# First pool group's gates as plain products in place of a seven-product scheme, in a two-layer trunk kernel

## Chip, cores and metric

The kernel runs on one core of a Trainium2 chip. The metric is the device time of one execution in microseconds (us). The kernel before took 920.03 us, the median of three runs (919.65 to 921.34).

## The reference, cut to what matters

The input is 512 tokens of width 1024, in float32. An even layer (matrix memory and stick-breaking attention) is followed by an odd layer, a pooling mixer. The change lies in the odd layer alone:

```python
def odd_layer(x, pre_g, post_g, w_in, pool_w, pool_scale, w_out):
    h = rmsnorm(x, pre_g)
    u = h @ w_in                                  # (512, 1024) @ (1024, 4096)
    p, z = u[..., :2048], u[..., 2048:]
    pooled = multiscale_pool(p in 4 groups of 512 channels)   # windows 2, 4, 8, 16: mean less the token
    mixed = einsum('bsgc,gce->bsge', pooled, pool_w)          # 512 x 512 per group
    y = (mixed * pool_scale * silu(z)) @ w_out
    return x + rmsnorm(y, post_g)
```

Here z holds the gates: 512 columns for each of the four groups.

## The kernel before, in words

Activations are kept transposed, 128 channels by 512 tokens, so that a product takes 128 weight columns as the stationary operand of TensorE and streams the tokens. Every float32 operand is split in two: a rounded half made by ScalarE (ACT, line 71) and the rest made by VectorE (DVE, line 72). `mm3` (lines 93 to 97) then issues three matmuls for each 128 by 128 block of weights. The normalised activations of the odd layer are `hTh` and `hTl`; the unsplit ones are kept in `y32`.

The odd layer goes through the four pool groups one after the other (loop at line 734). For a group it does five things:

- the projections p: two loads of 256 weight columns, four tiles of 128 columns, each tile eight blocks times three matmuls (`project2`, `col_proj`). In group 0 each tile is done in two token halves, since the second half of the tokens is normalised late (line 745). The results go to tiles `win` through line 748;
- the pooling: shifted sums on DVE (line 763), a small repair of the first tokens on GpSimd (POOL, lines 768 and 769), the rest on DVE (line 770), and the split in `pph` and `ppl`;
- the gates z: for each pair of column tiles `strassen2` (lines 688 to 732) forms the 256 by 512 result from seven products of half size (128 columns, half the channels, 256 tokens) in place of eight. It needs sums of the weights (lines 696 to 700, on DVE, then split) and sums of the activations;
- the load and split of the mixing weights `pw` (lines 783 and 784);
- the mixing itself, four tiles `mx` (lines 785 to 791), and line 792, which scales and gates.

The activation sums d3, d1, n2 and t4 are made once by `hidden_sums` (lines 672 to 686), four 128 by 1024 operations on DVE and four splits, and serve all eight gate pairs. Group 0 calls it behind its projections (line 749).

The program is written in this order, but a scheduler sets the order on each engine: it moves instructions by what they depend on and by its own cost estimates. Each engine then works strictly in its order. Loads are issued by SyncE's queue (SP) in order too; a load waits until its buffer is free. There are two load buffers (`w32`), four pairs of split weights (`wh`, `wl`), two banks `pj` for projections, and two banks `ac` for the mixing. Plain projections use the `pj` banks; `strassen2` uses one `pj` bank and two others (line 712).

Of the kernel before, what the change touches and what calls it, by code (L numbers as in the profile page):

```python
# [7 lines left out]
AF = mybir.ActivationFunctionType  # L8
# [28 lines left out]
def body(nc, tc, x, pre_g, post_g, w_in, conv, b_i, b_f, hn_g, w_out, w_in_c, pool_w,  # L37
# [6 lines left out]
    with base as base, psum as psum, dram as dram:  # L44
# [157 lines left out]
        with tc.tile_pool(name="att", bufs=1) as at:  # L202
# [374 lines left out]
            for u in range(HB // 2):  # L577
                pair = heads_b(u)
                stick_pair(pair, ((sc, sc), (xa, xb)))
                z = raw2(ZB + 256 * u, f"zb{u}")  # L580
# [46 lines left out]
        with tc.tile_pool(name="odd", bufs=1) as od:  # L627
# [44 lines left out]
            def hidden_sums():  # L672
                raw = {}
                b11, b21, b12, b22 = quarter(0, 0), quarter(1, 0), quarter(0, 1), quarter(1, 1)
                for n in ("d3", "d1", "n2", "t4"):
                    raw[n] = ws(f"raw_{n}").rearrange("p a n -> p (a n)").rearrange("p (a n) -> p a n", a=4)
                    hs[n] = [big(f"{n}{e}", F32R).rearrange("p (a n) -> p a n", a=4) for e in "hl"]
                    if n == "d3":
                        V.tensor_tensor(raw[n], b22, b12, op=ALU.subtract)
                    elif n == "d1":  # L680
                        V.tensor_tensor(raw[n], b11, b12, op=ALU.subtract)
                    elif n == "n2":
                        V.scalar_tensor_tensor(raw[n], raw["d3"], -1.0, b11, op0=ALU.mult, op1=ALU.subtract)
                    else:
                        V.scalar_tensor_tensor(raw[n], raw["n2"], -1.0, b21, op0=ALU.mult, op1=ALU.subtract)
                    split(raw[n], *hs[n])

            def strassen2(src, name, dsts, silu=False):

                w = load(lambda t: [(nc.sync, t, src)], 8, 256, name)  # L690
                a11, a12, a21, a22 = (w[:, 4 * k:4 * k + 4, m * P:m * P + P]
                                      for m in range(2) for k in range(2))
                sums = [ws(f"ws{i}_{name}") for i in range(2)]
                s1, s2, s3, s4 = sums[0][:, 4:], sums[0][:, :4], sums[1][:, :4], sums[1][:, 4:]
                first = halves(w[:, :, :P], f"{name}_a")
                V.tensor_tensor(s1, a21, a22, op=ALU.add)
                V.tensor_tensor(s2, s1, a11, op=ALU.add)
                second = halves(sums[0], f"{name}_b")
                V.tensor_tensor(s3, a11, a21, op=ALU.add)
                V.tensor_tensor(s4, a12, s2, op=ALU.add)  # L700
                third = halves(sums[1], f"{name}_c")
                fourth = halves(a22, f"{name}_d")

                def product(ps, wt, k0, b, start, stop):
                    (wh, wl), (bh, bl) = wt, hs[b]
                    for k in range(4):
                        mm3(ps, (wh[:, k0 + k], wl[:, k0 + k]), (bh[:, k], bl[:, k]),
                            start and k == 0, stop and k == 3, skip_group_check=True)

                def part(i): return od.tile([P, 256], F32, tag="part", bufs=4, name=f"pt{i}_{name}")  # L710

                pa, pb, pe = (f(f"ps{n}_{name}")[:, :256] for f, n in ((pj, "a"), (xa, "b"), (xb, "e")))
                t1, t2, t5 = part(1), part(2), part(5)
                product(pa, first, 0, "11", True, True)
                A.activation(t1, pa, AF.Copy)
                product(pb, first, 4, "21", True, True)
                V.tensor_tensor(dsts[0][:, :256], pb, t1, op=ALU.add)
                product(pa, second, 0, "n2", False, True)
                A.activation(t2, pa, AF.Copy)
                product(pe, second, 4, "d1", True, True)  # L720
                A.activation(t5, pe, AF.Copy)
                product(pa, third, 0, "d3", False, True)
                V.scalar_tensor_tensor(dsts[1][:, 256:], pa, -1.0, t5, op0=ALU.mult, op1=ALU.subtract)
                product(pe, third, 4, "22", False, True)
                V.tensor_tensor(dsts[0][:, 256:], pe, t2, op=ALU.add)
                product(pa, fourth, 0, "t4", False, True)
                if silu:
                    act(dsts[0], dsts[0], AF.Silu)
                    act(dsts[1][:, 256:], dsts[1][:, 256:], AF.Silu)
                    act(dsts[1][:, :256], pa, AF.Silu, scale=-1.0)  # L730
                else:
                    A.activation(dsts[1][:, :256], pa, AF.Copy, scale=-1.0)

            for g, w in enumerate(WINDOWS):
                pooled = []
                cur4 = []
                for j in range(4):
                    c = 4 * g + j
                    cur = od.tile([P, 16 + S], F32, tag="win", bufs=6, name=f"p_{c}")
                    G.memset(cur[:, :16], 0.0)  # L740
                    cur4.append(cur)
                wsrc = [w_in_c[0, :, 512 * g + 256 * i:512 * g + 256 * i + 256] for i in range(2)]
                if g == 0:
                    wj = [t() for i in range(2) for t in col_load(wsrc[i], f"p{g}{i}")]
                    for j, n0 in ((j, n0) for n0 in (0, 256) for j in range(4)):
                        ps = pj(f"ps_p{4 * g + j}_{n0}")
                        col_proj(wj[j], ps, n0, n0 + 256)
                        A.activation(cur4[j][:, 16 + n0:16 + n0 + 256], ps[:, n0:n0 + 256], AF.Copy)
                    hidden_sums()
                else:  # L750
                    for i in range(2):
                        for j, ps in enumerate(project2(wsrc[i], f"p{g}{i}")):
                            A.activation(cur4[2 * i + j][:, 16:], ps, AF.Copy)
                for j in range(4):
                    c = 4 * g + j
                    cur = cur4[j]
                    p32 = cur[:, 16:]
                    sh = 1
                    while sh < w:
                        nx = od.tile([P, 16 + S], F32, tag="win", bufs=6, name=f"p_{c}_{sh}")  # L760
                        if 2 * sh < w:
                            G.memset(nx[:, :16], 0.0)
                        V.tensor_tensor(nx[:, 16:], cur[:, 16:], cur[:, 16 - sh:16 + S - sh],  # L763
                                        op=ALU.add)
                        cur, sh = nx, 2 * sh
                    sm = cur[:, 16:]
                    e = w - 1
                    G.tensor_tensor(sm[:, :e], sm[:, :e], invc[:, :e], op=ALU.mult)  # L768
                    G.tensor_tensor(sm[:, :e], sm[:, :e], p32[:, :e], op=ALU.subtract)
                    V.scalar_tensor_tensor(sm[:, e:], sm[:, e:], 1.0 / w, p32[:, e:], op0=ALU.mult,  # L770
                                           op1=ALU.subtract)
                    ph = od.tile([P, S], F32R, tag="phi", bufs=5, name=f"pph{c}")
                    pl = od.tile([P, S], F32R, tag="plo", bufs=5, name=f"ppl{c}")
                    split(sm, ph, pl)
                    pooled.append((ph, pl))
                sz = []
                for i in range(2):
                    pair = [od.tile([P, S], F32, tag="sz", bufs=4, name=f"sz{4 * g + 2 * i + j}")
                            for j in range(2)]
                    strassen2(w_in_c[0, :, 2048 + 512 * g + 256 * i:2304 + 512 * g + 256 * i],  # L780
                              f"z{g}{i}", pair, True)
                    sz.extend(pair)
                w4 = load(lambda t: [(nc.sync, t, pool_w[0, g])], 4, 512, f"pw{g}")
                pw = [halves(w4[:, 2 * i:2 * i + 2], f"pw{g}{i}") for i in range(2)]
                for e in range(4):
                    c = 4 * g + e
                    ps = ac(f"mx{c}")
                    for k in range(4):
                        wh, wl = pw[k // 2]
                        mm3(ps, (wh[:, k % 2, e * P:e * P + P], wl[:, k % 2, e * P:e * P + P]),  # L790
                            pooled[k], k == 0, k == 3)
                    V.scalar_tensor_tensor(y32[:, c], ps, psc(c), sz[e], op0=ALU.mult, op1=ALU.mult)
# [44 lines left out]
```

## Time and profile before

| what | value |
|---|---|
| runs, median (lowest to highest) | 920.03 us (919.65 to 921.34) |
| the profiled execution's own time | 920.03 us |
| its span, first to last instruction | 918.0 us |
| TensorE matmul busy (share of the span) | 900.2 us (98%) |
| VectorE busy | 581.1 us (63%) |
| ScalarE busy | 491.2 us (54%) |
| GpSimd busy | 76.1 us (8%) |
| mean granted TensorE clock | 0.988 of full |

The span is 2.0 us shorter than the execution's own time; that remainder lies around the instructions. Busy time of TensorE counts a matmul from its start to its modelled end, and matmuls overlap, so what one costs is read from the distance between the starts of neighbours.

### The profile page before, as it was taken

The page shows a single profiled execution, that of the slowest core. Times are in us where ns is not written, and L with a number is a line of the kernel's source. Part 1 is how long each engine was busy: PE and PEld are TensorE (multiplying, and loading weights), DVE is VectorE, ACT ScalarE, POOL GpSimd, SP SyncE. Part 2 cuts the span into 40 slices and gives each one's busy share as a digit, 9 for nine tenths or more (in the row PEclk, how much of TensorE's full clock was granted, in tenths as well). Part 3 has the DMA queues.
Part 4 walks back from the last instruction along what each step waited for, and adds up shares of the span by engine and source line. Part 5 has one row for each costly group of instructions (what it writes and reads, how often), then busy time and mean ns, then how long its engine had stood idle before and what let it go on. Part 6 is the DMA issues. An engine that isn't in the chain of part 4 may idle for free.

```text
span 918.0 us, 12207 instructions
## 1 busy us (share of the span) xinstructions
PE 900.2 (98%) x4741; PEld 770.4 (84%) x4741; DVE 581.1 (63%) x865; ACT 491.2 (54%) x826; POOL 76.1 (8%) x221
## 2 busy tenths in 40 slices
PE   8999999999999999999999999997999999999996
PEld 6788889889988898898898878897889898988885
DVE  5435556567876675764864739589485776957542
ACT  6426666766668464464565537564344353455331
POOL 2001111101101101001000000004020110200000
PEclk8999999999999999999999999997999999999998
DMA  8231321212133323324221456611423233146321
GB/s 299 86 99 51 90 88 51 91 48 87 53 92 95 123 93 102 98 70 132 92 93 46 169 176 228 207 46 46 138 73 116 89 108 122 47 161 229 128 102 46
DMA packets 67130, 98.93 MB, mean 108 GB/s; under 512 B 2848, under 2 KB 54136, under 8 KB 67072
## 3 DMA queue, kind: packets, MB, share of 16 engines
q1 hardware_dynamic: 65888, 98.08, 32.7%
q8 instruction: 37, 0.61, 0.3%
q10 hardware_dynamic: 1184, 0.08, 0.1%
q14 instruction: 21, 0.17, 0.1%
HBM read 96.02 MB, written 2.13 MB: 107 GB/s over the span
## 4 chain that ended last, share of the span: by engine, by line
PE 88%; issue 8%; DVE 1%; POOL 1%; DMA 1%; ACT 0%; SPq 0%; DVEq 0%; POOLq 0%
PE oq L540 10%; PE op L540 5%; PE ps_qa L97 3%; PE ps_qa L96 3%; PE ps_qa L95 3%; PE ps_p L95 2%; PE ps_p L96 2%; PE ps_p L97 2%; PE psa_z L97 2%; PE psv_va L97 2%; PE psv_va L95 2%; PE psv_va L96 2%; PE psa_z L95 2%; PE psa_z L96 2%; PE ps_zb L95 2%
## 5 line engine op out<-in xcount | busy, mean ns | idle before, releaser
L96 PE MATMUL ps_p<-hTl,wh_p 128*128 128x512 f32 (+1 forms) x160 | 55.9, 350 | 0.2 <-DVE hTl L72 0.2
L95 PE MATMUL ps_p<-hTh,wh_p 128*128 128x512 f32 (+1 forms) x160 | 55.7, 350 | 0.0
L97 PE MATMUL ps_p<-hTh,wl_p 128*128 128x512 f32 (+1 forms) x160 | 55.6, 348 | 0.0
L97 PE MATMUL ps_qa<-hTh,wl_qa 128*128 128x512 f32 x128 | 50.3, 393 | 0.0
L95 PE MATMUL ps_qa<-hTh,wh_qa 128*128 128x512 f32 x128 | 50.2, 393 | 0.0
L96 PE MATMUL ps_qa<-hTl,wh_qa 128*128 128x512 f32 x128 | 50.2, 392 | 0.0
L72 DVE TENSOR_TENSOR wl_wo_e<-w_wo_e,wh_wo_e 128x1024 fp32r<-128x1024 f32 x28 | 34.3, 1233 | 23.4 <-ACT wh_wo_e L71 23.3
L71 ACT ACTIVATE wh_wo_e<-w_wo_e 128x1024 fp32r<-128x1024 f32 x28 | 29.4, 1058 | 29.0 <-DMA w_wo_e<-in_w_out_ab 12.2
L71 ACT ACTIVATE wh_p<-w_p 128x1024 fp32r<-128x1024 f32 x16 | 16.9, 1057 | 46.3 <-issue 26.1
L540 PE MATMUL op<-wh_wo_e,yl_e 128*128 128x512 f32 x120 | 39.1, 396 | 0.0
L540 PE MATMUL op<-wl_wo_e,yh_e 128*128 128x512 f32 x120 | 39.1, 396 | 0.0
L540 PE MATMUL op<-wh_wo_e,yh_e 128*128 128x512 f32 x120 | 37.8, 395 | 0.0
L67 ACT ACT_TABLE_LOAD x28 | 35.9, 1283 | 1.3 <-PEq L822 0.8
L97 PE MATMUL psv_va<-wh_va,hTl 128*128 128x256 f32 x128 | 36.1, 282 | 0.0
L95 PE MATMUL psv_va<-wh_va,hTh 128*128 128x256 f32 x128 | 36.1, 282 | 0.0
L96 PE MATMUL psv_va<-wl_va,hTh 128*128 128x256 f32 x128 | 36.1, 282 | 0.0
L320 DVE SCALAR_TENSOR_TENSOR cv<-u,vecs,cv 128x511 f32<-128x511 f32 (+2 forms) x48 | 35.4, 748 | 0.4
L96 PEld LDWEIGHTS ps_p<-hTl,wh_p 128*128 128x128 f32 x160 | 30.2, 189 | 4.3 <-DVE hTl L72 0.4
L97 PEld LDWEIGHTS ps_p<-hTh,wl_p 128*128 128x128 f32 x160 | 30.2, 189 | 4.1
L95 PEld LDWEIGHTS ps_p<-hTh,wh_p 128*128 128x128 f32 x160 | 30.1, 189 | 4.1
L72 DVE TENSOR_TENSOR wl_wo_o<-w_wo_o,wh_wo_o 128x1024 fp32r<-128x1024 f32 x20 | 24.3, 1223 | 12.5 <-ACT wh_wo_o L71 12.4
L768 POOL TENSOR_TENSOR p<-p,invc 128x1 f32<-128x1 f32 (+3 forms) x16 | 17.7, 1109 | 162.4 <-DVE p L763 162.3
(370 smaller groups left out, 2878.4 us busy)
## 6 DMA issues: line engine op xcount, KB each, us to landing
w_wo_e<-in_w_out_ab SPq DMA_DIRECT2D x14, 1024.0 KB, 4.9
w_wo_o<-in_w_out_c SPq DMA_DIRECT2D x12, 1024.0 KB, 4.9
w_qa<-in_w_in_ab SPq DMA_DIRECT2D x8, 1024.0 KB, 4.9
w_p<-in_w_in_c SPq DMA_DIRECT2D x8, 1024.0 KB, 5.6
w_z<-in_w_in_c SPq DMA_DIRECT2D x8, 1024.0 KB, 5.2
w_qb<-in_w_in_ab SPq DMA_DIRECT2D x4, 1024.0 KB
w_kb<-in_w_in_ab SPq DMA_DIRECT2D x4, 1024.0 KB, 5.0
w_zb<-in_w_in_ab SPq DMA_DIRECT2D x4, 1024.0 KB, 5.0
```

The source lines that it names most:

```text
L67: link(A.preload_act_table_set(TABLE[func]))
L71: A.activation(hi, src, AF.Copy)
L72: V.tensor_tensor(lo, src, hi.bitcast(F32), op=ALU.subtract)
L95: T.matmul(dst, lhsT=ah, rhs=bh, start=first, stop=False, **kw)
L96: T.matmul(dst, lhsT=ah, rhs=bl, start=False, stop=False, **kw)
L97: T.matmul(dst, lhsT=al, rhs=bh, start=False, stop=last, **kw)
L320: V.scalar_tensor_tensor(acc[:, j:], u[:, :S - j], cw(3 - j, c), acc[:, j:], op0=ALU.mult, op1=ALU.add)
L540: T.matmul(ps[a][n], lhsT=l[:, ta], rhs=r[:, 0, n * 512:n * 512 + 512], start=(first and l is yh and r is wh), stop=(last and l is yl))
L768: G.tensor_tensor(sm[:, :e], sm[:, :e], invc[:, :e], op=ALU.mult)
```

## The change

For group 0 alone the two gate pairs are made by `project2`, the plain way of the projections: per column tile eight blocks over all 512 tokens, and the SiLU reads the finished bank. The call of `hidden_sums` is written behind these gates and ahead of the mixing weights' load. Groups 1 to 3 keep `strassen2`.

```diff
                         A.activation(cur4[j][:, 16 + n0:16 + n0 + 256], ps[:, n0:n0 + 256], AF.Copy)
-                    hidden_sums()
                 else:
...
                 for i in range(2):
+                    zsrc = w_in_c[0, :, 2048 + 512 * g + 256 * i:2304 + 512 * g + 256 * i]
                     pair = [od.tile([P, S], F32, tag="sz", bufs=4, name=f"sz{4 * g + 2 * i + j}")
                             for j in range(2)]
-                    strassen2(w_in_c[0, :, 2048 + 512 * g + 256 * i:2304 + 512 * g + 256 * i],
-                              f"z{g}{i}", pair, True)
+                    if g == 0:
+                        for j, ps in enumerate(project2(zsrc, f"z{g}{i}")):
+                            act(pair[j], ps, AF.Silu)
+                    else:
+                        strassen2(zsrc, f"z{g}{i}", pair, True)
                     sz.extend(pair)
+                if g == 0:
+                    hidden_sums()
                 w4 = load(lambda t: [(nc.sync, t, pool_w[0, g])], 4, 512, f"pw{g}")
```

What this makes of the engines' orders is shown at three places. The first is VectorE from the first activation sum on (`raw_d`, `raw_n`, `raw_t` and `d3l` to `t4l` are the sums and their lower halves, `wl_z` lower halves of gate weights, `ws_z` sums of gate weights, `p_1` pool sums). Before:

```order
L679 TENSOR_TENSOR raw_d_5711<-y_65 128x1024
L681 TENSOR_TENSOR raw_d_5717<-y_65 128x1024
L683 SCALAR_TENSOR_TENSOR raw_n_5723<-raw_d_5711,y_65 128x1024
L72 TENSOR_TENSOR d3l<-raw_d_5711,d3h 128x1024
L72 TENSOR_TENSOR d1l<-raw_d_5717,d1h 128x1024
L72 TENSOR_TENSOR wl_z_a<-w_z_5773,wh_z_a 128x1024
L685 SCALAR_TENSOR_TENSOR raw_t_5729<-raw_n_5723,y_65 128x1024
L763 TENSOR_TENSOR p_1_5735<-p_5475 128x512
L72 TENSOR_TENSOR n2l<-raw_n_5723,n2h 128x1024
L696 TENSOR_TENSOR ws_z_5775<-w_z_5773 128x512
L763 TENSOR_TENSOR p_1_5744<-p_5477 128x512
```

The same place with the change, from the fourth sum on and a few rows further:

```order
L685 SCALAR_TENSOR_TENSOR raw_t_5894<-raw_n_5888,y_65 128x1024
L762 TENSOR_TENSOR p_1_5711<-p_5475 128x512
L72 TENSOR_TENSOR n2l<-raw_n_5888,n2h 128x1024
L72 TENSOR_TENSOR wl_z_1_5784<-w_z_5749,wh_z_1_5783 128x1024
L762 TENSOR_TENSOR p_1_5720<-p_5477 128x512
L72 TENSOR_TENSOR wl_z_0_5818<-w_z_5814,wh_z_0_5817 128x1024
L769 SCALAR_TENSOR_TENSOR p_1_5711<-p_1_5711,p_5475 128x511
L72 TENSOR_TENSOR t4l<-raw_t_5894,t4h 128x1024
L72 TENSOR_TENSOR wl_z_1_5848<-w_z_5814,wh_z_1_5847 128x1024
L769 SCALAR_TENSOR_TENSOR p_1_5720<-p_1_5720,p_5477 128x511
L762 TENSOR_TENSOR p_1_5729<-p_5479 128x512
```

The rows ahead of these are the same as before: the activation sums keep their place at the front. All four lower halves of the gate weights now stand ahead of the third pool sum, and the sums of weights are gone.

The second place is TensorE where gate products lie among the projections and the mixing (`ps_p_256` are projections of the second token half, `psb_z` one of the seven products, `ps_z` the new gate tiles, `mx` the mixing). Before:

```order
L97 MATMUL ps_p_256_5633<-hTh,wl_p_1_5490 128x256
L95 MATMUL psb_z_5798<-hTh,wh_z_a 128x256
L96 MATMUL psb_z_5798<-hTl,wh_z_a 128x256
L95 MATMUL ps_p_256_5659<-hTh,wh_p_0_5495 128x256
L96 MATMUL ps_p_256_5659<-hTl,wh_p_0_5495 128x256
L97 MATMUL ps_p_256_5659<-hTh,wl_p_0_5496 128x256
```

With the change, between the first and the second gate pair:

```order
L96 MATMUL ps_z_1_5782<-hTl,wh_z_1_5783 128x512
L97 MATMUL ps_z_1_5782<-hTh,wl_z_1_5784 128x512
L95 MATMUL mx_5910<-pph_5716,wh_pw_5902 128x512
L95 MATMUL mx_5924<-pph_5716,wh_pw_5902 128x512
L95 MATMUL ps_z_0_5816<-hTh,wh_z_0_5817 128x512
L96 MATMUL ps_z_0_5816<-hTl,wh_z_0_5817 128x512
```

No gate product stands among the projections any more, and one matmul of each of the first two mixing tiles now stands between the two gate pairs.

The third place is ScalarE around the first pooled tile `pph` (`pt_z`, `wh_z_b` to `wh_z_d` belong to the seven products, `wh_pw` to the mixing weights, `sz` is a SiLU). Before:

```order
L748 ACTIVATE p_5481<-ps_p_256_5685 128x256
L715 ACTIVATE pt_z_5800<-psa_z_5797 128x256
L71 ACTIVATE pph_5740<-p_1_5735 128x512
L71 ACTIVATE wh_z_b<-ws_z_5775 128x1024
L71 ACTIVATE pph_5749<-p_1_5744 128x512
L71 ACTIVATE wh_z_c<-ws_z_5776 128x1024
```

With the change:

```order
L748 ACTIVATE p_5481<-ps_p_256_5685 128x256
L71 ACTIVATE pph_5716<-p_1_5711 128x512
L71 ACTIVATE wh_pw_5902<-w_pw_5900 128x1024
L68 ACTIVATE sz_5747<-ps_z_0_5751 128x512
L71 ACTIVATE pph_5725<-p_1_5720 128x512
L71 ACTIVATE pph_5734<-p_1_5729 128x512
L71 ACTIVATE wh_pw_5906<-w_pw_5900 128x1024
L68 ACTIVATE sz_5748<-ps_z_1_5782 128x512
```

The split of the mixing weights moved up to right behind the first pooled tile, ahead of the SiLU that empties the first gate bank.

## Rows read from the trace of the kernel before

**Rows 1.** The page: busy time and instructions by engine; TensorE's busy share and granted clock in 40 slices of the span, in tenths; the chain of work that ended last, by engine.

```profile
PE 900.2 (98%) x4741; PEld 770.4 (84%) x4741; DVE 581.1 (63%) x865; ACT 491.2 (54%) x826; POOL 76.1 (8%) x221
PE   8999999999999999999999999997999999999996
PEclk8999999999999999999999999997999999999998
PE 88%; issue 8%; DVE 1%; POOL 1%; DMA 1%; ACT 0%; SPq 0%; DVEq 0%; POOLq 0%
```

**Rows 2.** Busy time by stretch. Columns: the stretch, its length, busy us (instructions) of TensorE, its weight loads, VectorE, ScalarE and GpSimd, then the granted TensorE clock, DMA share and GB/s. The first two stretches run from the first gate product to the first projection of group 1, and from there to the last matmul; the others lie inside the first.

```profile
621.49:655.44 33.95, 28.94 (x192) 27.37 (x191) 25.59 (x37) 17.20 (x28) 7.76 (x13) 0.85 0.29 94
655.44:910.98 255.54, 255.50 (x1345) 217.61 (x1343) 163.02 (x218) 104.60 (x159) 19.24 (x55) 1.00 0.34 112
...
624.10:636.41 12.31, 7.30 (x34) 6.86 (x33) 11.96 (x19) 7.37 (x11) 5.04 (x12) 0.59 0.03 11
...
635.00:636.00 1.00, 1.00 (x7) 1.00 (x7) 1.00 (x2) 1.00 (x2) 0.00 (x0) 0.50 0.29 98
...
637.00:638.00 1.00, 1.00 (x11) 1.00 (x10) 1.00 (x2) 0.00 (x0) 0.08 (x1) 1.00 0.98 356
```

**Rows 3.** Waits of TensorE between 600 and 660 us: who waited for whom, us in total, times, the longest.

```profile
PE psa_z L95 <- ACT wh_z_b L71: 3.2, 1, 3.2
PE psa_z L97 <- DVE wl_z_b L72: 1.8, 1, 1.8
```

**Rows 4.** TensorE in order of time. Columns: start, duration, engine, line, operation with its tiles and shape, and in brackets idle time before it and what ended it.

```profile
614.93 0.28 PE L97 MATMUL ps_p<-hTh,wl_p 128*128 128x256 f32 x1
615.38 0.39 PE L95 MATMUL psb_z<-hTh,wh_z_a 128*128 128x256 f32 x1 [0.17 <-ACT wh_z_a L71]
...
615.72 0.32 PE L95 MATMUL ps_p<-hTh,wh_p 128*128 128x256 f32 x1
...
621.49 0.28 PE L95 MATMUL psa_z<-hTh,wh_z_a 128*128 128x256 f32 x1
...
623.98 0.28 PE L97 MATMUL psb_z<-hTh,wl_z_a 128*128 128x256 f32 x1
627.43 0.58 PE L95 MATMUL psa_z<-n2h,wh_z_b 128*128 128x256 f32 x1 [3.17 <-ACT wh_z_b L71]
...
630.48 0.58 PE L97 MATMUL psa_z<-n2h,wl_z_b 128*128 128x256 f32 x1 [1.83 <-DVE wl_z_b L72]
...
646.99 0.39 PE L95 MATMUL mx<-pph,wh_pw 128*128 128x512 f32 x1
...
650.72 0.28 PE L95 MATMUL pse_z<-hTh,wh_z_c 128*128 128x256 f32 x1
...
653.58 0.39 PE L97 MATMUL mx<-pph,wl_pw 128*128 128x512 f32 x1
...
655.44 0.40 PE L95 MATMUL ps_p<-hTh,wh_p 128*128 128x512 f32 x1
```

**Rows 5.** VectorE in order of time, the same columns.

```profile
610.93 1.23 DVE L679 TENSOR_TENSOR raw_d<-y 128x1024 f32<-128x1024 f32 x1 [0.66 <-ACT y L184]
612.07 1.22 DVE L681 TENSOR_TENSOR raw_d<-y 128x1024 f32<-128x1024 f32 x1
...
618.88 0.69 DVE L763 TENSOR_TENSOR p<-p 128x512 f32<-128x512 f32 x1
619.48 1.22 DVE L72 TENSOR_TENSOR n2l<-raw_n,n2h 128x1024 fp32r<-128x1024 f32 x1
620.62 0.69 DVE L696 TENSOR_TENSOR ws_z<-w_z 128x512 f32<-128x512 f32 x1
...
625.80 0.69 DVE L763 TENSOR_TENSOR p<-p 128x512 f32<-128x512 f32 x1 [0.35 <-POOL p L769]
...
627.07 0.42 DVE L717 TENSOR_TENSOR sz<-psb_z,pt_z 128x256 f32<-128x256 f32 x1
627.40 0.68 DVE L696 TENSOR_TENSOR ws_z<-w_z 128x512 f32<-128x512 f32 x1
...
629.21 1.22 DVE L72 TENSOR_TENSOR wl_z_b<-ws_z,wh_z_b 128x1024 fp32r<-128x1024 f32 x1
...
633.88 0.69 DVE L72 TENSOR_TENSOR wl_z_d<-w_z,wh_z_d 128x512 fp32r<-128x512 f32 x1
```

**Rows 6.** ScalarE in order of time, the same columns.

```profile
615.23 0.37 ACT L748 ACTIVATE p<-ps_p 128x256 f32<-128x256 f32 x1
...
625.80 0.63 ACT L71 ACTIVATE pph<-p 128x512 fp32r<-128x512 f32 x1 [2.31 <-POOL p L769]
626.34 1.04 ACT L71 ACTIVATE wh_z_b<-ws_z 128x1024 fp32r<-128x1024 f32 x1
...
667.56 0.58 ACT L753 ACTIVATE p<-ps_p 128x512 f32<-128x512 f32 x1
```

**Rows 7.** GpSimd in order of time, the same columns.

```profile
619.65 5.85 POOL L768 TENSOR_TENSOR p<-p,invc 128x1 f32<-128x1 f32 x1 [71.85 <-DVE p L763]
625.58 0.19 POOL L769 TENSOR_TENSOR p<-p,p 128x1 f32<-128x1 f32 x1
```

**Rows 8.** The queue of loads in order of time, the same columns, and for the loads issued by line 83 between 580 and 720 us the time from issue to landing.

```profile
591.77 8.10 SPq L83 DMA_DIRECT2D w_z<-in_w_in_c  x2
634.60 0.37 SPq L83 DMA_DIRECT2D w_pw<-in_pool_w  x1
...
DMA to landing us min/median/max: 5.0/5.4/6.4
```

## The prediction

> **What bounds the kernel now.** I read the page first: TensorE is busy for 98% of the span, it carries 88% of the chain that ended last, and only one slice inside the span, the 28th of 40, drops to 7, in the busy share and in the granted clock alike [rows 1]. A slice is 918.0 / 40 = 22.95 us, so the 28th is 620 to 643 us. Cutting the time by stretch shows what it is: from 621.49 us (first gate product of group 0) to 655.44 us (first projection of group 1) the granted clock is 0.85, while in the 255.54 us behind it TensorE is busy for 255.50 us at clock 1.00 [rows 2]. Behind group 0, then, nothing but TensorE's work counts, and what group 0 gains is kept to the end. The waits name the cause: 3.2 us for the upper half of the weight sums (wh_z_b, ScalarE) and 1.8 us for their lower half (wl_z_b, VectorE) [rows 3]. In order of time TensorE issues its 22nd gate product of the stretch at 623.98, then waits to 627.43 and again to 630.48 [rows 4]. After the first of these waits it works at half clock, 0.50 (the 1.2 GHz level of the two), and is back at 1.00 by 637 [rows 2]. Why the sums were late shows on VectorE: it has no gap from 610.93 to 625.45 and is busy for 11.96 of the 12.31 us between 624.10 and 636.41 [rows 2, 5]. The stage is VectorE's: activation sums, weight sums, splits and pooling stand in one line, and wl_z_b begins only at 629.21, with TensorE wanting it at 624.1.
>
> **The prices.** Sixteen mixing matmuls of 512 tokens start between 646.99 and 650.72: 3.73 / 16 = 0.2331 us each. The 24 gate products of 256 tokens behind them, 650.72 to 653.58, take 2.86 / 24 = 0.1192 us each [rows 4]. These are distances between starts at full clock, which is what a matmul costs here. On VectorE a 128x1024 operation takes 1.14 us from start to start (610.93 to 612.07), a 128x512 one 0.60 (618.88 to 619.48) and a 128x256 combination 0.33 (627.07 to 627.40) [rows 5].
>
> **What is removed and added on TensorE.** The seven-product scheme has 7 products x 4 blocks x 3 matmuls = 84 per pair, 168 for two pairs, 168 x 0.1192 = 20.03 us at full clock. The plain way has 4 tiles x 8 blocks x 3 = 96 matmuls of 512 tokens, 96 x 0.2331 = 22.38 us. Taken by itself this edit costs 2.35 us.
>
> **What the stretch takes now.** Before 655.44 lie 166 gate products (two of the 168 were issued at 615, inside another wait) and the 24 matmuls of the first two mixing tiles: 166 x 0.1192 + 24 x 0.2331 = 19.79 + 5.59 = 25.38 us of work in 33.95 us [rows 2]. Lost are 8.57 us: 5.0 us of named waits [rows 3], the rest the half clock and the restarts.
>
> **What it takes with the change.** If TensorE never waits, the same stretch is 96 + 24 = 120 matmuls, 120 x 0.2331 = 27.97 us. The difference is 33.95 - 27.97 = 5.98 us. The start of the stretch stays at 621.49: the two products that stood at 615 were in the shadow of a wait for the bank that line 748 empties from 615.23 on, and the third projection tile resumes at 615.72 with or without them [rows 4, 6].
>
> **Does TensorE wait?** Projected starts from 621.49: first gate tile, second at 627.1, two mixing matmuls at 632.7, third tile at 633.1, fourth at 638.7, the other 22 mixing matmuls at 644.3, end at 649.5. Against that:
>
> - VectorE. The change drops, per pair, three 1024-wide and one 512-wide split, four 512-wide sums and three combinations (3 x 1.14 + 5 x 0.60 + 3 x 0.33 = 7.4 us), and adds two 1024-wide splits (2.3 us): 10.2 us less over both pairs. The activation sums have not moved: in the new order they head the line as before. From 619.48 on, adding the prices along the new rows, the second tile's lower half is done at 621.8 (wanted at 627.1), the third's at 623.6 (633.1), the fourth's at 626.5 (638.7). Spare time 5 to 12 us, where before it was short by 6. Group 1 is the first to use the activation sums, some 40 us later, so they may stand anywhere.
> - The banks. The first gate tile needs the bank of the third projection tile. That is emptied by ScalarE behind the split of the third gate tile's weights, which needs the weight buffer of the same projection tile. That tile's products end at about 615.72 + 24 x 0.1192 = 618.6; a split of 1.04 and a copy of 0.37 later [rows 6] it is 620.0. TensorE asks at 621.49: 1.5 us to spare, the thinnest place. Were the split a whole instruction later, one of 1.0 us, it would still hold.
> - The mixing weights. Their load waits for the first gate pair's load buffer. Before, that was let go by wl_z_d, which ended at 634.6, and the load was issued at that moment, 634.60 [rows 5, 8]. Now the last reader is the second tile's split, done at 621.8; landing takes 5.0 to 6.4 us [rows 8], so 627 to 628.3. The split (1.04) ends by 629.4, wanted at 632.7: 3.3 us to spare. Loads queued behind it for group 1 move up as well.
> - ScalarE drops ten activations per pair (four splits, three copies, three SiLUs) and gains four (two splits, two SiLUs of 128x512, priced by the 0.58 us of a copy of that size out of a bank [rows 6]). It was 17.20 us busy in 33.95 [rows 2] and stays under that.
>
> The operations added are all of kinds the trace shows; only the waits are unpriced. From below I bound them at nothing, and a further gain at 0.7 us (the whole stretch without work from 614.93 + 0.12 to 615.72 [rows 4], in case a copy comes earlier there). From above I bound them at 3 us: one wait like the longest one before (3.2 us) [rows 3] less some of its spare time, which would bring part of the half clock back. I take nothing, since each wait has 1.5 us or more to spare.
>
> **The sum.** The profiled execution took 920.03 us, which is also the median; its span is 918.0. 920.03 - 5.98 = 914.05: I predict 914.1 us.
>
> **GpSimd and the vector line.** The first small operation on GpSimd takes 5.85 us, from 619.65 to 625.5, and ends when VectorE stops to wait for it at 625.45 [rows 5, 7]; the one behind it takes 0.19. It looks as if it were held while VectorE runs without a gap. The Trainium skill, GPSIMD Engine Reference, section "Key points", says that GpSimd shares its SBUF interfaces with VectorE and contends with vector instructions that have two SBUF inputs. By that rule the trace agrees, 5.85 us for one column of data, though it shows it at one place only. In the new order VectorE runs on without a gap to the third pool sum at 627.0, 1.5 us longer. By the rule or by the row alone the sum stays at 914.1, since VectorE stops there by itself; what more holding would cost is rival A.
>
> **The rivals.**
>
> A. GpSimd is held longer. The first pooled tile waits for it on ScalarE [rows 6], and in the new order the mixing weights' split and the SiLU that empties the first gate bank queue behind it. At 627.0 VectorE itself waits, so the hold ends: pooled tile 627.4 to 628.0, split to 629.0, SiLU to 629.6, with TensorE asking at 632.7 and 633.1. Held twice as long (11.7 us, to 631.4), the split ends at 633.2 and the SiLU at 633.8, a wait of about 1.1 us: 915.2. If further pairs are held in turn and the clock falls again (some 3.6 us, the 8.57 less the 5.0 of waits), up to 918.5. For it: two-input operations fill VectorE. Against it: the next GpSimd operation took 0.19 us, and VectorE stops by itself for every second one.
>
> B. Slower than before: the mixing's first matmuls block TensorE. They now stand between the gate pairs, and TensorE works in order, so late mixing weights stop the second pair too. If the load still came at 634.60, it would land at 640 (5.4), be split by 641, and TensorE would wait from 632.7 to 641, 8.3 us, then run at half clock, 3.6: 914.1 + 11.9 = 926. It decides from 6.0 us of wait. For it: the load was 13 us later before than it has to be. Against it: it was let go by an instruction that the change removes [rows 5, 8].
>
> C. No difference: the waits go, but a new one takes about 4 to 8 us, say at the bank with 1.5 us to spare, because ScalarE's order runs late as a whole: 918.2 to 921.9. Against it: ScalarE is half idle in the stretch [rows 2].
>
> That the change does not do what it says is true of the sums, which stand where they stood. But the gain does not come from them.
>
> **How the numbers follow.** Forecast 0.83, with its own range 913.2 to 915.2. A 0.09, 915.2 to 918. C 0.03. B 0.03. Better than 913.2 (the 0.7 us gain, and the runs' spread) 0.02. The range 912.9 to 916.8 takes in the forecast and the nearer half of A, and the runs' spread of up to 1.3 us above their median. 0.2% is 1.8 us, about what a measurement of this kernel tells from no change. Faster by more: the forecast, A and the better case, 0.94; within: C, 0.03; slower: B, 0.03.
>
> **What would show it.** Right: the stretch from the first gate product to group 1's first projection takes 28.0 us with the clock at 1.00 throughout; TensorE's waits for weight halves in it are gone; TensorE has 72 matmuls fewer; the load of the mixing weights is issued near 622; behind the stretch 255.5 us as before. Wrong: a wait at a gate tile's bank or at the first mixing matmul, a clock under 1.00 between 621 and 650, or a stretch behind group 0 that is longer than 256 us.

## The result and the profile after

The changed kernel took 914.26 us, the median of six runs (913.54 to 915.49), beside 920.07 us for the kernel before (919.49 to 921.34, six runs): a ratio of 0.9938, with a 95% interval of 0.9925 to 0.995. The prediction was 914.1. The profiled execution took 914.12 us, with a span of 912.2.

The page of the changed kernel, the same four lines as [rows 1]:

```profile
PE 897.8 (98%) x4669; PEld 764.9 (84%) x4669; DVE 570.6 (63%) x847; ACT 485.6 (53%) x814; POOL 77.3 (8%) x221
PE   7999999999999999999999999999999999999996
PEclk8999999999999999999999999999999999999999
PE 96%; DVE 1%; ACT 1%; DMA 1%; issue 0%; SPq 0%; DVEq 0%; POOL 0%; POOLq 0%; ACTq 0%
```

The dip in the 28th slice is gone from both rows, the chain is TensorE's for 96% in place of 88%, and TensorE has 4741 - 4669 = 72 matmuls fewer. By stretch, against [rows 2] (from the first gate product to group 1's first projection, then to the last matmul):

```profile
621.68:649.40 27.72, 27.72 (x122) 22.56 (x121) 16.09 (x20) 9.71 (x14) 9.69 (x13) 1.00 0.40 128
...
649.40:905.10 255.70, 255.63 (x1345) 217.64 (x1343) 162.28 (x216) 104.71 (x159) 18.26 (x55) 1.00 0.33 110
```

The stretch went from 33.95 to 27.72 us, at a granted clock of 1.00 in place of 0.85, and what lies behind it kept its length to 0.16 us (255.70 for the same 1345 matmuls, 255.54 before). All of the gain is in group 0. TensorE's waits from 600 to 910 us, against [rows 3], and its starts at the joints of the stretch, against [rows 4]:

```profile
PE ps_p L95 <- ACT p L748: 0.4, 1, 0.4
PE tp_p L179 <- ACT y L184: 0.3, 1, 0.3
PE ps_p L96 <- DVE hTl L72: 0.2, 1, 0.2
```

```profile
615.85 0.39 PE L95 MATMUL ps_p<-hTh,wh_p 128*128 128x256 f32 x1 [0.43 <-ACT p L748]
...
621.68 0.39 PE L95 MATMUL ps_z<-hTh,wh_z 128*128 128x512 f32 x1
...
632.74 0.63 PE L95 MATMUL mx<-pph,wh_pw 128*128 128x512 f32 x2
...
649.40 0.39 PE L95 MATMUL ps_p<-hTh,wh_p 128*128 128x512 f32 x1
```

No wait for a half of weights is left. The three that remain lie ahead of the stretch. The four places that the prediction had named as thin stand as follows; ScalarE first, then GpSimd and the queue of loads:

```profile
619.85 0.36 ACT L748 ACTIVATE p<-ps_p 128x256 f32<-128x256 f32 x1
...
627.59 0.63 ACT L71 ACTIVATE pph<-p 128x512 fp32r<-128x512 f32 x1 [4.50 <-POOL p L768]
628.13 1.05 ACT L71 ACTIVATE wh_pw<-w_pw 128x1024 fp32r<-128x1024 f32 x1
629.08 0.58 ACT L68 ACTIVATE sz<-ps_z 128x512 f32<-128x512 f32 x1
```

```profile
619.85 7.45 POOL L767 TENSOR_TENSOR p<-p,invc 128x1 f32<-128x1 f32 x1 [71.84 <-DVE p L762]
627.37 0.19 POOL L768 TENSOR_TENSOR p<-p,p 128x1 f32<-128x1 f32 x1
```

```profile
622.06 0.37 SPq L83 DMA_DIRECT2D w_pw<-in_pool_w  x1
```

The bank is emptied at 620.21, 1.47 us ahead of TensorE's 621.68. The mixing weights are asked for at 622.06 (634.60 before) and their first split ends at 629.18, 3.56 us ahead of the mixing's first matmul. ScalarE stood still for 4.50 us behind GpSimd, and nobody missed it.

### The profile page after: what moved, and what is told of

Read it like the earlier page. It is cut to its first block, busy times and chain, and to the rows that moved or that the text cites. A ratio compares the mean times of both kernels' runs of the same rounds, so it can differ in the third digit from the quotient of the medians.

```text
span 912.2 us, 12027 instructions
## 1 busy us (share of the span) xinstructions
PE 897.8 (98%) x4669; PEld 764.9 (84%) x4669; DVE 570.6 (63%) x847; ACT 485.6 (53%) x814; POOL 77.3 (8%) x221
## 4 chain that ended last, share of the span: by engine, by line
PE 96%; DVE 1%; ACT 1%; DMA 1%; issue 0%; SPq 0%; DVEq 0%; POOL 0%; POOLq 0%; ACTq 0%
PE op L540 10%; PE oq L540 10%; PE ps_qa L97 3%; PE ps_qa L95 3%; PE ps_qa L96 3%; PE ps_p L95 3%; PE ps_p L97 3%; PE ps_p L96 3%; PE psv_va L95 2%; PE psv_va L97 2%; PE psv_va L96 2%; PE ps_zb L95 2%; PE mx L96 2%; PE mx L97 2%; PE mx L95 2%; PE ps_oa L96 2%
```

## The experiments

Three accounts were to be told apart. Mine: before, TensorE waited in group 0 because VectorE had too much to do in one line ahead of the halves that TensorE wanted; plain products take that work away at a price of 2.35 us. A first rival: the waits came from GpSimd, which held the pooled tile and behind it ScalarE's splits. A second: the place of the activation sums has a share in the gain. All runs in one table. "Stage" is read from each trace: from group 0's first projection matmul to group 1's first, 594.80 to 655.44 in the kernel before and 595.00 to 649.40 with the change. What follows the stage, to the end of the span, took 262.6 to 263.3 us in all but three kernels (the first, the second and the fifth experiment), so a difference in the stage is the difference that counts. The median is that of all runs of a kernel, the stage that of one execution, the profiled one.

| kernel | median us | ratio to before, interval | stage us |
|---|---|---|---|
| before | 920.07 to 920.50 in the five sessions | | 60.64 |
| the change | 914.26 | 0.9938 [0.9925, 0.995] | 54.40 |
| the change again | 914.32 | 0.9938 [0.9926, 0.9951] | 54.41 |
| 1 no weight sums | 912.99 | 0.9921 [0.9908, 0.9933] | other order |
| 2 groups 0 and 1 plain | 916.57 | 0.9958 [0.9946, 0.9971] | 54.40 |
| 3 first pair plain | 913.59 | 0.9924 [0.9912, 0.9937] | 53.31 |
| 4 weights ahead of pooling | 916.21 | 0.9958 [0.9944, 0.9971] | 55.61 |
| 5 sums behind the mixing | 915.32 | 0.9944 [0.9932, 0.9957] | 53.96 |
| 6 change, repair on VectorE | 914.76 | 0.9939 [0.9927, 0.9952] | 54.37 |
| 7 before, repair on VectorE | 917.78 | 0.9979 [0.9969, 0.9988] | 58.10 |
| 8 second pair plain | 920.63 | 0.9999 [0.999, 1.0008] | 60.10 |
| 9 early weight sums | 916.00 | 0.9957 [0.9943, 0.997] | 55.58 |
| 10 the same, repair on VectorE | 915.26 | 0.9947 [0.9934, 0.9959] | 54.40 |
| 12 sums in the gaps | 915.81 | 0.9942 [0.9928, 0.9955] | 56.02 |

### 1. Seven products without their sums of weights

```diff
-                sums = [ws(f"ws{i}_{name}") for i in range(2)]
...
+                if name.startswith("z0"):
+                    second = third = fourth = halves(w[:, :, P:], f"{name}_b")
```

> Group 0 keeps the seven products of the kernel before, but no sums of weights are formed: the second, third and fourth weight sets are all the split of the plain second column tile (this part of the computation is left out). VectorE then splits two weight sets per pair, as with the change, while TensorE keeps 168 short matmuls. Theory (waits for weight sums cost 8.6 us, plain products cost 2.35 us more than seven): no long wait, 920.1 - 8.6 = 911.5, up to 912.5 with a short wait of a part's copy; about 2.4 us under the changed kernel. Rival 1 (the plain products are as cheap as the seven on this chip): the same as the changed kernel, 914.3. Rival 2 (the activation sums, not the weight sums, were late): the wait at the products with n2 and d1 stays, over 916.

Measured: 912.99. No wait for a half over 0.3 us is left in group 0; the longest is one for the mixing weights:

```profile
PE mx L95 <- ACT wh_pw L71: 0.5, 1, 0.5
```

So the 168 short matmuls go through group 0 without a long wait, once the weight sums are gone and with them half of the weight splits, on VectorE and on ScalarE alike. It is half a us above the expected range, and 1.3 under the change where 2.4 had been expected.

### 2. Group 1 plain too

```diff
-                    if g == 0:
+                    if g <= 1:
                         for j, ps in enumerate(project2(zsrc, f"z{g}{i}")):
```

> The changed kernel with the gates of group 1 plain too. Theory: group 1 had no wait of TensorE, so only the price of the plain products comes, 914.3 + 2.35 = 916.6 (916.0 to 917.2). Rival (what helped was less work on VectorE and ScalarE as such): 914.3 or less.

Measured: 916.57, which is 2.31 over the change; 2.35 was worked out for one group's plain products. Those two medians come from different sessions. In the traces, group 0's stage is unchanged at 54.40, and from group 1's first projection to group 3's first the change and this kernel take

```profile
649.40:756.09 106.69, 106.69 (x626) 94.15 (x625) 72.85 (x100) 44.20 (x68) 11.74 (x37) 1.00 0.30 96
```

```profile
649.34:758.10 108.76, 108.76 (x553) 92.16 (x552) 63.05 (x82) 39.14 (x56) 10.12 (x37) 1.00 0.30 94
```

which is 2.07 us more. Where nothing waits, the plain way costs just its matmuls.

### 3. Plain products for the first pair alone

```diff
-                    if g == 0:
+                    if g == 0 and i == 0:
...
-                if g == 0:
-                    hidden_sums()
+                    if g == 0 and i == 0:
+                        hidden_sums()
```

> Only the first gate pair of group 0 is plain; the second has seven products. Theory: the plain pair is cover enough; VectorE, followed row by row, has the second pair's weight sums split at about 631.6 us, and TensorE wants them at 635.5, so no wait and half the extra price is saved: 914.3 - 1.2 = 913.1. Rival (VectorE's line is too long again): a wait at the second pair's sums or at the mixing, 915 to 918.

Measured: 913.59, and the stage 1.09 us shorter than with the change (half of 2.35 is 1.18), with the clock at 1.00 throughout:

```profile
595.30:648.61 53.31, 52.35 (x365) 48.35 (x364) 42.67 (x59) 30.67 (x52) 12.21 (x13) 1.00 0.29 90
```

Its waits are the same three, of 0.4, 0.3 and 0.2. The lower median is in line with that, though the two intervals overlap.

### 4. Before, with the weights ahead of the pooling

```diff
+                        if g == 0:
+                            tc.add_manual_dep(i.ins, mark["z00"].name, NOSYNC, reason="weights first")
```

The dependency puts group 0's pool sums behind the split of the first pair's third weight set. The gates of group 0 are also written ahead of its pooling, which the cut above does not show.

> The kernel before, all groups with seven products, with nothing changed but VectorE's order in group 0: a dependency without a semaphore holds the pool sums behind the third weight set's split of the first pair. Theory (VectorE's order, not its total work, made the wait): the sums' lower half starts near 625.4 instead of 629.2, TensorE waits about 2 us instead of 5 and the clock may stay full: 912.5 to 915, that is as good as the change or better. Rival (VectorE has too much work in this stretch in any order): the wait goes to the mixing, 917 to 921.

Measured: 916.21, over the 915 of the theory and under the 917 of the rival. The upper half comes nearly in time, the lower one still late. TensorE's rows, ScalarE's split of the upper half (2.4 us earlier than in [rows 6]), and ten us of the stretch, in which the clock holds:

```profile
625.04 0.39 PE L97 MATMUL psa_z<-n2h,wh_z_b 128*128 128x256 f32 x1 [0.23 <-ACT wh_z_b L71]
627.13 0.38 PE L99 MATMUL psa_z<-n2h,wl_z_b 128*128 128x256 f32 x1 [1.35 <-DVE wl_z_b L72]
...
632.41 0.39 PE L99 MATMUL psa_z<-hTh,wl_z_a 128*128 128x256 f32 x1 [0.74 <-DVE wl_z_a L72]
```

```profile
623.94 1.05 ACT L71 ACTIVATE wh_z_b<-ws_z 128x1024 fp32r<-128x1024 f32 x1
```

```profile
624.00:634.00 10.00, 7.67 (x60) 7.07 (x60) 9.89 (x15) 6.07 (x10) 2.22 (x4) 1.00 0.27 88
```

VectorE is busy for 9.89 of these 10.00 us. Even with the pooling out of the way its line is too long for both pairs. Yet order alone, with every operation kept, takes 5.03 us off the stage. Not all of that is VectorE's: ScalarE's split of the upper half no longer stands behind a pooled tile, the first of which is split only at 633.05, so GpSimd's share goes in this run too. The seventh experiment tells the two apart.

### 5. The activation sums really moved

```diff
                 if g == 0:
-                    hidden_sums()
...
                     V.scalar_tensor_tensor(y32[:, c], ps, psc(c), sz[e], op0=ALU.mult, op1=ALU.mult)
+                if g == 0:
+                    hidden_sums()
```

> The changed kernel with the call of hidden_sums written behind group 0's mixing, so that three of the four sums really leave group 0 on VectorE (some 9 us of its work: three sums and three lower halves go to group 1). Theory (group 0 is bounded by TensorE's 120 matmuls in the changed kernel, so VectorE's work there may come or go): 914.3, within 0.5 of the changed kernel, stretch of about 27.8 us. Rival (VectorE is still what sets group 0): faster by 1 us or more. Other rival (the sums are missed in group 1): a wait of TensorE there, 916 or more.

In this kernel the sums read activations that line 795 has meanwhile replaced by mixed ones, so groups 1 to 3 take their gates from other data. The sums really left: from 600 to 660 us VectorE is busy for 31.43 us instead of 40.02. Measured: 915.32, which is 1.06 over the change and outside the half us expected. The stage is 0.44 shorter, all of it ahead of the stretch, where TensorE's wait of 0.43 for the bank is gone; in the stretch VectorE is busy for 11.38 us instead of 16.09. Then group 1 takes back more than that, with the wait of the other rival:

```profile
622.73:650.45 27.72, 27.72 (x123) 22.55 (x121) 11.38 (x14) 8.66 (x12) 2.58 (x9) 1.00 0.35 107
```

```profile
685.39 0.39 PE L95 MATMUL psa_z<-d3h,wh_z_c 128*128 128x256 f32 x1 [1.06 <-ACT pt_z L719]
```

From the first gate product on the stretch is 27.72 us again, to the hundredth. The second rival falls: the place of the sums gives nothing that group 1 does not take back.

### 6 and 7. The first-token repairs on VectorE, with the change and before

```diff
-                    G.tensor_tensor(sm[:, :e], sm[:, :e], invc[:, :e], op=ALU.mult)
-                    G.tensor_tensor(sm[:, :e], sm[:, :e], p32[:, :e], op=ALU.subtract)
+                    R = V if g == 0 else G
+                    R.tensor_tensor(sm[:, :e], sm[:, :e], invc[:, :e], op=ALU.mult)
+                    R.tensor_tensor(sm[:, :e], sm[:, :e], p32[:, :e], op=ALU.subtract)
```

> The changed kernel with the repair of the first tokens in group 0 made by VectorE, not GpSimd, so that nothing can be held on GpSimd. Theory (the hold of 7.45 us on GpSimd has some 3 us to spare there): 914.3, within 0.5 of the changed kernel, no new wait. Rival A (the hold costs something in the changed kernel): faster by 0.5 us or more.

> The kernel before with the same repair on VectorE. Now ScalarE's split wh_z_b needn't stand behind a pooled tile that waits for GpSimd. Theory (GpSimd's hold with ScalarE's strict order made a part of the 3.2 us wait, VectorE's own line the rest): wait for wh_z_b shorter by about 1.4 us, wait for wl_z_b about 2.2 in place of 1.8, together 4.0 in place of 5.0; 918 to 920. Rival (the wait is all of VectorE's making): no change, 920.0 to 920.7. Rival (it is all GpSimd's): both waits go, 915 or less.

Measured: 914.76 with the change, no gain, stage 54.37. Rival A had no price. But before, the same edit gives 2.7 us between the medians (917.78), 1.9 by the ratio, with an interval from 1.1 to 2.9; the profiled stage is 2.54 shorter. The same two waits as [rows 3], in order of time, and ScalarE's split that no longer stands behind a pooled tile:

```profile
626.00 0.38 PE L95 MATMUL psa_z<-n2h,wh_z_b 128*128 128x256 f32 x1 [1.81 <-ACT wh_z_b L71]
...
628.99 0.39 PE L97 MATMUL psa_z<-n2h,wl_z_b 128*128 128x256 f32 x1 [2.26 <-DVE wl_z_b L72]
```

```profile
624.88 1.06 ACT L71 ACTIVATE wh_z_b<-ws_z 128x1024 fp32r<-128x1024 f32 x1 [1.46 <-DVE ws_z L697]
```

The first wait is 1.36 shorter, since the split starts at 624.88 instead of 626.34 [rows 6]; the second is 0.43 longer. Neither rival holds alone: GpSimd made a part of the loss, VectorE's line the greater rest. The run came out a little better than the 918 to 920 expected, because the clock was down for a shorter time, from about 629.3 to 632.7, by these rows of single us:

```profile
629.00:630.00 1.00, 1.00 (x6) 1.00 (x7) 1.00 (x2) 1.00 (x2) 0.11 (x1) 0.65 0.00 0
630.00:631.00 1.00, 1.00 (x6) 1.00 (x6) 1.00 (x4) 0.21 (x1) 0.00 (x0) 0.50 0.00 0
...
632.00:633.00 1.00, 1.00 (x8) 1.00 (x8) 1.00 (x2) 0.00 (x0) 0.00 (x0) 0.64 0.00 0
```

Five of its nine executions, with a mean granted clock of 0.992 to 0.994, took 917.51 to 917.78; the four with 0.991 took 918.50 to 919.88. In the kernel before the clock had been down from about 626.2, while TensorE still stood in its first wait, to about 636.4:

```profile
626.00:627.00 1.00, 0.00 (x0) 0.00 (x0) 1.00 (x2) 1.00 (x2) 0.90 (x2) 0.60 0.00 0
...
636.00:637.00 1.00, 1.00 (x8) 1.00 (x8) 1.00 (x3) 0.33 (x2) 0.03 (x1) 0.78 0.68 164
```

### 8. Plain products for the second pair alone

```diff
-                    if g == 0:
+                    if g == 0 and i == 1:
```

> Seven products for group 0's first gate pair, plain products for its second (and the sums of activations where the kernel before has them). Theory (both waits belong to the first pair's sums of weights, ahead of which only one sum of 0.6 us goes): the wait for wh_z_b stays at about 3.2, that for wl_z_b falls to about 1.2, the clock falls again, and the plain pair costs 1.2 of TensorE: 919.5 to 921. Rival (it is the total of VectorE's work in the stretch that counts, whichever pair it comes from): half of the gain or more, 917 or less.

Measured: 920.63, no gain at all, with the waits as written down:

```profile
629.01 0.58 PE L95 MATMUL psa_z<-n2h,wh_z_b 128*128 128x256 f32 x1 [3.15 <-ACT wh_z_b L71]
...
631.46 0.58 PE L97 MATMUL psa_z<-n2h,wl_z_b 128*128 128x256 f32 x1 [1.23 <-DVE wl_z_b L72]
```

Beside the third experiment this is the clearest pair: the same number of operations goes from VectorE, yet taken from the first pair they bring 6.9 us and from the second none. What stands ahead of the wanted half in VectorE's line decides, not VectorE's total.

### 9 to 11. Seven products kept, the first pair's weight sums made early, and the change beside them

```diff
                     wj = [t() for i in range(2) for t in col_load(wsrc[i], f"p{g}{i}")]
+                    made0 = weight_sums(w_in_c[0, :, 2048:2304], "z00")
...
-                              f"z{g}{i}", pair, True)
+                              f"z{g}{i}", pair, True, made0 if g == 0 and i == 0 else None)
```

`weight_sums` holds the load and the four sums of `strassen2`, unchanged.

> The kernel before, seven products kept everywhere, but the four sums of the weights of group 0's first gate pair are written ahead of its projections, so that VectorE makes them around 598 to 603 us, before the activation sums exist (four buffers for sums in place of three, and four in place of five for the pooled halves, to make room). Theory (before lost its 8.6 us because these sums stood behind activation sums and pooling in VectorE's line, not because the seven products are too dear for TensorE): the waits for wh_z_b and wl_z_b go, the clock stays at 1.00, TensorE keeps the 2.35 us that the plain products cost, less up to 2 us if the 2.4 us of sums delay the normalisation between 598 and 611: 912 to 914. Rival (with seven products VectorE has too much in this stretch wherever the sums stand): waits of 2 us or more on other halves, 915 or more.

> The same with the first-token repairs of group 0 on VectorE, so that no pooled tile waits for GpSimd. Theory (with the weight sums early, ScalarE's order is no longer held up where TensorE wants something): within 0.7 of the run with early weight sums alone. Rival (GpSimd's hold still costs there, as it did before the change): 1 us or more faster than that run.

> The changed kernel itself, beside the two others on one chip: 914.3, within 0.7.

Measured: 916.00, 915.26 and 914.32. The ninth kernel missed its 912 to 914, and the tenth is 0.74 us faster than the ninth, between the 0.7 of its theory and the 1 of its rival. The waits for `wh_z_b` and `wl_z_b` are gone, so the order was what made them late. But the sums now delay the normalisation, and TensorE waits there, for the transposes; this wait has the same length in both kernels:

```profile
609.86 1.62 PE L179 MATMUL tp_p<-ident,xse 128*128 128x128 f32 x8 [1.91 <-ACT y L184]
```

The bound of 2 us that I gave for this took no account of the clock, which fell behind the wait in the ninth kernel. In the profiled execution of the tenth the clock stayed up, and the stage is 54.40, level with the change: the matmuls saved pay for the new wait. But of the tenth kernel's five executions only two, this one and another, had a mean granted clock of 0.995 and took 914.12 and 914.22; three had 0.993 and took 915.26 to 916.25. So its median, 0.94 over that of the change, belongs to an execution with the lower clock.

### 12. The sums in the gaps of the normalisation

```diff
+                i = V.tensor_tensor(s1, a21, a22, op=ALU.add)
+                if name == "z00":
+                    tc.add_manual_dep(i.ins, mark["norm"].name, NOSYNC, reason="norm first")
```

The same for the third sum; the rest is the tenth kernel.

> The kernel with early weight sums and repairs on VectorE, but the four sums held behind the last normalising operation (line 174 before), where VectorE has gaps of 2.1, 1.3 and 0.7 us in the kernel before. Theory (the 1.9 us that TensorE waited for the transposes with early weight sums came from the sums standing ahead of the normalisation, and nothing else is left to wait for): that wait goes, the clock stays at 1.00, TensorE keeps the 2.35 us of the plain products: 912 to 913, below the changed kernel. Rival (VectorE is too full behind 611 to make the seven products' halves in time even so): a new wait of 1 us or more for a half, 914 or more.

Measured: 915.81, over the 912 to 913 of the theory, and the rival was right. The wait for the transposes is gone, but now an activation sum is late:

```profile
627.98 0.39 PE L96 MATMUL psa_z<-n2l,wh_z_b 128*128 128x256 f32 x1 [1.34 <-DVE n2l L72]
```

The clock fell once more, and VectorE works without a gap over 0.1 us from 612.57 to beyond 640:

```profile
631.00:632.00 1.00, 1.00 (x6) 1.00 (x6) 1.00 (x4) 0.00 (x0) 0.00 (x0) 0.50 0.56 188
```

This execution took 916.24. The two with a mean granted clock of 0.995 and 0.996 took 914.28 and 913.93, about level with the change, the three with 0.992 and 0.993 took 915.81 to 916.43. With seven products for both pairs of group 0, every order tried (before and the fourth, the ninth, the tenth and the twelfth experiment) left something late; of the kernels that do the whole work, only those with plain products for the first pair have no wait over 0.5 us. That the third experiment with some further order would do better is not excluded; it wasn't tried.

## Why the prediction was right

- What bounds the kernel: right. Group 0's waits and the half clock were the whole difference; the rest stayed as it was.
- The price of the plain products, 2.35 us: right, a little high. At the 0.2310 us a matmul that the new stretch shows, 96 take 22.18 us and the price is 2.15; the second experiment's traces show 2.07 (its median 2.31), the third's stage 1.09 for half.
- The stretch without a wait, 120 matmuls at 0.2331 = 27.97 us: measured 27.72, or 0.2310 each. The gain in it is 6.23 in place of 5.98; the stretch began 0.19 later than before, as did what lies ahead of it, and what follows took 0.16 longer. That the sum came within 0.2 us of the median is in part luck, as these small misses cancel.
- The spare times: the bank 1.5 us (1.47 measured), the mixing weights' load near 622 (622.06), their split ready by 629.4 (629.18), the new hold on GpSimd ending at about 627.0 (627.30). All of them came out of adding up durations along the new order, which is why the sum could stand without an allowance for waits.
- The half clock: priced with the waits as lost time that goes whole. It went: no wait in the new stage is longer than 0.43 us, and the clock is 1.00 throughout the stretch.
- One reason was told too simply: "The stage is VectorE's". The seventh experiment shows that of the 8.57 us lost some 2 to 2.5, the shorter time at half clock included, hung on the repairs on GpSimd, with ScalarE's split queued behind the pooled tile. [rows 6] had it: the pooled tile stood 2.31 us idle behind GpSimd, and the split right behind it ended the wait of 3.17. The forecast was not hurt, as the change removes that split whoever made it late.
- The sums: that they "may stand anywhere" and that the gain doesn't come from them holds for the order on VectorE; the fifth experiment moved them and gained nothing, though in group 1 they were no longer free (1.06 us).

## What to carry to other kernels

A scheme that saves matmuls pays only where the engine that prepares its operands has room: in the first of four groups it saved some 2.2 us of matmuls and lost 8.57 us in waits and half clock. Order alone, without a plain product, took back 5.0 and 5.1 us of the stage (the fourth and the ninth experiment). Look not for the busiest engine but for what stands ahead of the late operand in that engine's line, and also on the engine that is to issue the operand's other half; removing equal work behind it gives nothing. And follow the new order with measured durations before trusting a sum without waits: that left little to guess in this one.

## What was not expected

**The clock behind a wait.** The granted clock fell to 0.50, the 1.2 GHz level, within the wait of 3.17 us in the kernel before and within that of 3.15 in the eighth experiment, but also behind waits of 1.81 and 2.26 in the seventh and of 1.34 and 0.47 in the twelfth; it stayed at 1.00 with 1.35 and 0.74 in the fourth. The same wait of 1.91 us at the same place went either way. One us of the ninth and the tenth kernel, behind that wait:

```profile
612.00:613.00 1.00, 1.00 (x5) 1.00 (x6) 0.69 (x1) 0.73 (x3) 0.00 (x0) 0.50 0.00 0
```

```profile
612.00:613.00 1.00, 1.00 (x10) 1.00 (x10) 0.34 (x2) 0.91 (x2) 0.00 (x0) 1.00 0.00 0
```

In the same time TensorE starts 5 matmuls or 10. The ninth kernel's stage is 1.18 us longer than the tenth's; that the clock is the cause fits, but the two differ in the repairs as well. These begin only at 620 us, behind the fall at about 610.4, so they did not make it. And the runs of the tenth kernel alone part by their mean granted clock, 0.995 or 0.993, as told above. What decides whether the clock falls behind a wait of one or two us, these runs don't tell.

**GpSimd's hold.** The one-column operation took 5.85 us before and in the eighth experiment, 7.45 with the change, 8.12 in the third, each time until VectorE itself stood waiting for it. I had read this as a hold for as long as VectorE runs without a gap. That is not the whole of it: in the ninth experiment the same operation came through under a VectorE without a gap:

```profile
620.12 1.10 POOL L773 TENSOR_TENSOR p<-p,invc 128x1 f32<-128x1 f32 x1 [71.67 <-DVE p L768]
...
628.87 2.85 POOL L773 TENSOR_TENSOR p<-p,invc 128x1 f32<-128x1 f32 x1 [4.18 <-DVE p L768]
```

```profile
631.59 0.42 DVE L721 TENSOR_TENSOR sz<-psb_z,pt_z 128x256 f32<-128x256 f32 x1
```

The second of these ended at 631.72, 0.13 us after VectorE had begun an operation that takes one of its two inputs from a bank of results. From 600 us on the traces hold 27 repair operations on GpSimd that took 1.5 us or more. Five ended so, 0.13 to 0.14 us into such an operation (7.45 us in the first experiment, 2.31 in the fourth, 2.92 in the fifth, 2.85 and 2.30 in the ninth), the other 22 when VectorE had nothing running.

The Trainium skill, GPSIMD Engine Reference, section "Key points", names contention with vector instructions that have two SBUF inputs (SBUF is the memory that holds the tiles; the banks of results are another). By that rule the runs agree, as every long hold ended where VectorE no longer ran an operation with both inputs in that memory. But why the operation of 1.10 us, and one of 0.57 in the fourth experiment, came through between such operations and another took 8.12, neither the rule nor these runs say. On VectorE the same operation took 0.15 us.

**Where scatter of the runs comes from.** Group 0 began at anything from 594.73 us (seventh experiment) to 596.49 (fifth) in the profiled executions, ahead of the stage that the edits change. Comparing a stage by its own ends, as the table does, resolves differences of a few tenths that the medians, with runs of one kernel up to 3.1 us apart, do not. That holds where the clock stays up, as in the change (54.40 and 54.41). Where it falls, how far differs from one execution to the next: in one session the kernel before took 918.28 us at a mean granted clock of 0.995 and 921.02 and 921.10 at 0.988.
